# A gated hybrid decoder step: sampled values spread by selecting matmuls, and four state tiles

## The chip, the cores and the metric

The kernel runs on one core of a Trainium2 chip. The metric is the device time of one execution in microseconds (us); a timing is the median of several runs. The core has five engines with queues of their own that run beside each other and meet at semaphores: PE (TensorE, matmuls), DVE (VectorE), ACT (ScalarE), POOL (GpSimd, here mainly an issuer of DMAs) and SP (SyncE, the other issuer of DMAs). Each takes its instructions in order: one that waits holds those behind it.

## The reference

One layer of a decoder whose mixer has two branches on the same normalised input, retention and RWKV-7, for two sets of tokens: a prompt of 512 tokens that starts from zero states, and eight sampled tokens (one of each of eight sequences) that start from given states. All inputs and outputs are fp32.

```python
D_MODEL = 1024; SEQ = 512; DEC_BATCH = 8; RET_HEADS = 4; RET_DK = 256; RET_DV = 512

def chunk(s, qkv):                         # retention, one chunk of one head
    qc, kc, vc = qkv
    inner = jnp.einsum('bhid,bhjd->bhij', qc, kc) * dmask
    o = jnp.einsum('bhij,bhjv->bhiv', inner, vc) + jnp.einsum('bhid,bhdv->bhiv', qc * q_dec, s)
    s = chunk_dec * s + jnp.einsum('bhjd,bhjv->bhdv', kc * k_dec, vc)
    return s, o
...
o = o * lax.rsqrt(jnp.mean(o * o, axis=-1, keepdims=True) + NORM_EPS)
return o * jax.nn.silu(g_a), s             # the retention branch
...
def step(s, inp):                          # RWKV-7, one token
    r_t, w_t, k_t, v_t, kk_t, a_t = inp
    sk = jnp.einsum('bhvk,bhk->bhv', s, kk_t)
    s = s * w_t[:, :, None, :] - sk[..., None] * (a_t * kk_t)[:, :, None, :] + v_t[..., None] * k_t[:, :, None, :]
    return s, jnp.einsum('bhvk,bhk->bhv', s, r_t)
...
merged = sigmoid(m_a) * (y_a @ w_down_a) + sigmoid(m_b) * (y_b @ w_down_b)
x = x + merged @ w_out
x = x + (p @ w_ple) * sigmoid(_rmsnorm(x) @ w_ple_gate)
```

For a sampled token the retention state of one head, 256 by 512 values for each of eight sequences (4 MB), is multiplied by the head's decay, gets the outer product of the new key and value added, is written out, and is multiplied by the query. All eight states of four heads make 16 MB in and 16 MB out.

## The kernel before, in words

The work runs in three stages on one core. Stage A (to about 275 us) normalises and transposes the input, makes the RWKV projections and prepares per-chunk matrices, which it stores to memory. Stage B (to about 770 us) goes through the four retention heads. Stage C runs the RWKV chunks between the remaining projections, then the output projection, the gate and the final norm.

Every fp32 product is made as three fp32r products: an operand is split in a rounded part `hi` and a rest `lo`, and `hi·hi`, `hi·lo`, `lo·hi` are summed in PSUM. A weight block of 1024x128 is fetched by SP into one of three `raw` tiles, split by ACT (`whi`, L142) and DVE (`wlo`, L143), and used by 48 matmuls (L155), two halves of the tokens with 24 each, in four PSUM banks of the pool `ph`. One such block is called a projection here. Other results on PE go through three banks of the pool `px`, handed out by `bank()`; the sampled result has a bank `po` of its own.

A head in stage B makes, in this order in the code: the projections and rotation of k and q (two each, `rope`), four projections of v (`values`), the scores (`sc`, L776, split to `ihi` and `ilo`), transposes of v (`vt`, split to `vhi` and `vlo`), of the sampled v (`vs`) and of k (`kt`, split to `dhi` and `dlo`), the sampled states (`sampled`), four projections of the gate g_a (`gs`, in the slots of v), in the heads 2 and 3 also four projections of another gate, the output (`o`, L827, evacuated to `ot`), the new prompt state (`st`, L839), the transposes of `ot` (L846), the product with the gate (`y`, L848) and its store (`YAd`), and last `sampled_out`. The code's order is a priority, not the order on the engines: instructions are placed by a planner that simulates the engines and transfers ahead of time, each engine's list is fixed then, and the semaphores do the rest.

`sampled(h)` handles the 4 MB in four tiles of 1 MB: two groups `g` of four sequences, two halves `i` of the key dimension. Before the change the eight sampled value rows (512 values each) are written to memory (`VSd`, L797) and loaded again by a DMA that repeats them over all 128 partitions (`vb` in the tile `tv`, L690, 1 MB for each group, one slot, shared with `on` of `sampled_out`). The state tiles `tS` have two slots (L694); POOL issues their loads (L695) and stores (L705). ACT multiplies a tile by the decay (L698), DVE adds key times value (L699, with the key as the scalar of each partition), and PE multiplies by the query into `po` (L701). `after(m_, last)` makes the first of four po matmuls wait for the last state update before it.

Beside this, the generator `beside()` hands out DVE work in small pieces: first `solve()`, a triangular solve in the tile `M` (L615, L617) whose result is stored by SP (`TTd`), then `rwkv_sampled()`, which loads the RWKV states of the sampled tokens into the same slot `M` (L638) and updates them with nine DVE instructions for each of four parts (L643 to L660). `advance()` is called after each projection of k, q, v and g_a and takes pieces off the generator until a 42nd part of the whole work is paid for:

```python
def advance(share=1.0 / 42):
    nonlocal due
    due += share * WORK
    with tc.issue_after(marks[1]):
        while due > 0:
            w_ = next(extra, None)
            if w_ is None:
                break
            due -= w_ + 60
```

`issue_after(marks[1])` places those DVE instructions behind the latest weight split.

Of the kernel before, what the change touches and what calls it, by code (L numbers as in the profile page):

```python
# [8 lines left out]
F32 = mybir.dt.float32  # L9
F32R = mybir.dt.float32r  # L10
# [69 lines left out]
def body(tc, A, O, dbg=None, upto="Z"):  # L80
# [11 lines left out]
    with es:  # L92
# [24 lines left out]
        BNd = dr.tile([NPAIR, 128, NT], F32, tag="BNd", name="BNd")  # L117
        SMd = dr.tile([6, B8, D], F32, tag="SMd", name="SMd")
        OSd = dr.tile([128, 64], F32, tag="OSd", name="OSd")
        VSd = dr.tile([B8, H, DV], F32, tag="VSd", name="VSd")  # L120
        GBd = dr.tile([KT, 128, NT], F32, tag="GBd", name="GBd")
        UAd = dr.tile([KT, 128, NT], F32, tag="UAd", name="UAd")
        YBd = dr.tile([KT, 128, NT], F32, tag="YBd", name="YBd")
# [486 lines left out]
        def solve():  # L610
            for s in range(1, C - 1):
                n = C - 1 - s
                tm = pB.tile([128, 1024], F32, tag="tm", name="tm", bufs=1)
                tv = tm[:, 0:s * n].rearrange("p (i t) -> p i t", t=n)
                dve.tensor_tensor(tv, M[:, 0:s, s:s + 1].to_broadcast([128, s, n]),  # L615
                                  M[:, s:s + 1, s + 1:C].to_broadcast([128, s, n]), ALU.mult)
                dve.tensor_tensor(M[:, 0:s, s + 1:C], M[:, 0:s, s + 1:C], tv, ALU.add)  # L617
                yield s * n
            dve.memset(M.rearrange("p s t -> p (s t)")[:, 0::C + 1], 1.0)
            for c in range(NCH):  # L620
                sp.dma_start(TTd[c].rearrange("t h u -> h t u"), M[c * 16:(c + 1) * 16])
            yield 0
# [10 lines left out]
        def rwkv_sampled():  # L633
            S_ = pB.tile([128, C, C], F32, tag="M", name="S_")
            for q in range(C // HQ):
                vsl = slice(q * HQ, (q + 1) * HQ)
                S = S_[:, vsl]
                pool.dma_start(S, A["state_rwkv"][0].rearrange("b h v k -> (b h) v k")[:, vsl])  # L638
                tm = pB.tile([128, HQ, C], F32, tag="tm", name="rT", bufs=1)
                sk = pB.tile([128, HQ], F32, tag="rk", name="rk", bufs=1)  # L640
                kb = lambda i: sv[:, i:i + 1, :].to_broadcast([128, HQ, C])
                vb = lambda t: t.unsqueeze(2).to_broadcast([128, HQ, C])
                dve.tensor_tensor(tm, S, kb(4), ALU.mult)  # L643
                yield HQ * C / 2
                dve.tensor_reduce(sk, tm, AX.X, ALU.add)
                yield HQ * C / 2
                dve.tensor_tensor(S, S, kb(1), ALU.mult)
                yield HQ * C / 2
                dve.tensor_tensor(tm, vb(sk), kb(5), ALU.mult)
                yield HQ * C / 2  # L650
                dve.tensor_tensor(S, S, tm, ALU.subtract)
                yield HQ * C / 2
                dve.tensor_tensor(tm, vb(sv[:, 3, vsl]), kb(2), ALU.mult)
                yield HQ * C / 2
                dve.tensor_tensor(S, S, tm, ALU.add)
                yield HQ * C / 2
                pool.dma_start(O[6][0].rearrange("b h v k -> (b h) v k")[:, vsl], S)
                dve.tensor_tensor(tm, S, kb(0), ALU.mult)
                yield HQ * C / 2
                dve.tensor_reduce(os_[:, vsl], tm, AX.X, ALU.add)  # L660
                yield HQ * C / 2
            pool.dma_start(OSd, os_)

        def beside():
            yield from solve()
            yield from rwkv_sampled()

        extra = beside()
# [2 lines left out]
        def advance(share=1.0 / 42):  # L671
# [3 lines left out]
            with tc.issue_after(marks[1]):  # L675
                while due > 0:
# [2 lines left out]
                        break  # L679
                    due -= w_ + 60  # L680

        def sampled(h):
            qz = pR.tile([128, 2, 4, 34], F32, tag="qz", name="qz", bufs=1)
            dve.memset(qz, 0.0)
            dve.tensor_copy(qz[:, :, :, 0], qs[:, h, :, 0:4])
            dve.tensor_copy(qz[:, :, :, 33], qs[:, h, :, 4:8])
            po = pq.tile([128, 512], F32, tag="po", name="po")
            for g in range(2):
                vb = pR.tile([128, 4, DV], F32, tag="tv", name="tv", bufs=1)
                pool.dma_start(vb, VSd[4 * g:4 * g + 4, h, :].unsqueeze(0).to_broadcast([128, 4, DV]))  # L690
                for i in range(2):

                    src = slice(4 * g, 4 * g + 4)
                    S = pR.tile([128, 4, DV], F32, tag="tS", name="tS", bufs=2)  # L694
                    pool.dma_start(S, A["state_ret"][0, src, h, 128 * i:128 * i + 128, :].rearrange("b p v -> p b v"))  # L695
                    n_ = 32 if g == 0 and i == 0 else 2
                    for b in range(4):
                        act.activation(S[:, b, :], S[:, b, :], AF.Copy, scale=GAM[h])  # L698
                        last = dve.scalar_tensor_tensor(S[:, b, :], vb[:, b, :], ks[:, h, i, 4 * g + b:4 * g + b + 1], S[:, b, :], ALU.mult, ALU.add)  # L699
                    for b in range(4):  # L700
                        m_ = pe.matmul(po[32 * b:32 * b + n_, :], qz[:, i, b, 32 * g:32 * g + n_], S[:, b, :],  # L701
                                       start=(n_ == 32), stop=(g == 1 and i == 1), skip_group_check=True)
                        if b == 0:
                            after(m_, last)
                    pool.dma_start(O[5][0, src, h, 128 * i:128 * i + 128, :].rearrange("b p v -> p b v"), S)  # L705
            return po

        def sampled_out(h, po):
            on = pR.tile([128, DV], F32, tag="tv", name="on", bufs=1)
            os2 = small.tile([128, 2], F32, tag="os2", name="os2")  # L710
            act.activation(on, po, AF.Square, accum_out=os2[:, 0:1])
            rsqrt(os2[:, 1:2], os2[:, 0:1], 1.0 / DV, NORM_EPS)
            act.activation(on, po, AF.Copy, scale=os2[:, 1:2])
            ps = bank("yas")
            for i in range(4):
                pe.transpose(ps[:, 128 * i:128 * i + 128], on[:, 128 * i:128 * i + 128], ident)
            hs_ = slice(4 * h, 4 * h + 4)
            dve.tensor_tensor(yaS[:, hs_, :].rearrange("p i (g b) -> p i b g", g=2),
                              ps.rearrange("p (i b r) -> p i b r", i=4, b=4)[:, :, :, 0:2],
                              gs8[:, hs_, :].rearrange("p i (g b) -> p i b g", g=2), ALU.mult)  # L720
# [3 lines left out]
        for h in range(H):  # L724
# [61 lines left out]
            for jt in range(4):  # L786
                ps = bank("vt")
                for i in range(4):
                    pe.transpose(ps[:, 128 * i:128 * i + 128], vT[i][:, 128 * jt:128 * jt + 128], ident)
                act.activation(vhi[:, jt, :], ps, AF.Copy)  # L790
                dve.tensor_tensor(vlo[:, jt, :], ps, vhi[:, jt, :], ALU.subtract)
            ps = bank("vs")
            for i in range(4):
                pe.transpose(ps[0:B8, 128 * i:128 * i + 128], vT[i][:, T:NT], ident)
            vs = pB.tile([B8, DV], F32, tag="s_", name="vs", bufs=1)
            act.activation(vs, ps[0:B8, :], AF.Copy)
            pool.dma_start(VSd[:, h, :], vs)  # L797
            dhi = pB.tile([128, 4, 256], F32R, tag="khi", name="dhi")
            dlo = pB.tile([128, 4, 256], F32R, tag="klo", name="dlo")
            for jt in range(4):  # L800
# [17 lines left out]

            oss = pB.tile([128, 4], F32, tag="oss", name="oss", bufs=2)
            ort = pB.tile([128, 4], F32, tag="ort", name="ort", bufs=2)  # L820
            ot = []
            for it in range(4):
                ps = bank("o")
                seq = [(jt, a_, b_) for jt in range(it + 1) for a_, b_ in ((ihi, vhi), (ihi, vlo), (ilo, vhi))]
                for x, (jt, a_, b_) in enumerate(seq):
                    o_ = OFF[jt] + 128 * (it - jt)
                    pe.matmul(ps, a_[:, o_:o_ + 128], b_[:, jt, :], start=(x == 0), stop=(x == len(seq) - 1))  # L827
                o = pB.tile([128, DV], F32, tag="ot", name="ot", bufs=4)
                act.activation(o, ps, AF.Square, accum_out=oss[:, it:it + 1])
                act.activation(o, ps, AF.Copy)  # L830
                ot.append(o)
            rsqrt(ort, oss, 1.0 / DV, NORM_EPS)
            for it in range(4):
                act.activation(ot[it], ot[it], AF.Copy, scale=ort[:, it:it + 1])
# [8 lines left out]
            for i in range(4):  # L843
                ps = bank("ot")
                for it in range(4):
                    pe.transpose(ps[:, 128 * it:128 * it + 128], ot[it][:, 128 * i:128 * i + 128], ident)  # L846
                y = pB.tile([128, T], F32, tag="y", name="y", bufs=2)
                dve.tensor_tensor(y, ps, gs[i][:, 0:T], ALU.mult)  # L848
                sp.dma_start(YAd[4 * h + i], y)
            sampled_out(h, po)  # L850
        advance(1.0)
# [376 lines left out]
```

## Time and profile before

| | |
|---|---|
| median of three runs | 1140.19 us (1139.5 to 1141.54) |
| the profiled execution | 1142.53 us, span 1140.6 us |
| mean granted clock of PE | 0.969 |
| busy share PE, DVE, ACT, POOL | 93%, 68%, 44%, 6% |
| DMA | 211.1 MB, mean 185 GB/s |
| state loads, state stores, value loads | 16, 16 and 8 DMAs of 1 MB |

The profile is of one execution, slower than the median by 2.3 us. A row of the timeline gives the start, the duration, engine, line, operation, output and inputs, shapes and count, and in brackets the idle time of the engine before it and what ended that. A row of the table of waits gives who waited for whom, the total, the number of times and the longest. A row of the table of stretches gives start and end, length, busy time and number of instructions for each engine, then the granted clock of PE as a share of its full speed, the share of the DMA engines in use, and the rate in GB/s. PE matmuls overlap each other: their duration is longer than the distance of their starts, and the distance is what one costs.

### The profile page before, as it was taken

What the parts mean: (1) busy time and instruction counts of PE and PEld (TensorE: products, weight loads), DVE (VectorE), ACT (ScalarE), POOL (GpSimd) and SP (SyncE); (2) the same over time, 40 slices, a digit from 0 to 9 for tenths busy, and PEclk for the clock granted to TensorE, in tenths of its full rate; (3) what the DMA queues carried; (4) which work ended last, traced back from release to release, by engine and by line L of the source; (5) the groups of instructions that cost most, each with busy time, mean ns of one, the idle gap of its engine ahead of it and who ended that gap; (6) DMA issues with size and microseconds to landing.
All of it is one profiled execution on the core that took longest, in us unless ns stands there. A gap on an engine that the chain in (4) does not pass through costs nothing. (4 is left out here: it accounts for less than half of the span.)

```text
span 1140.6 us, 22817 instructions
## 1 busy us (share of the span) xinstructions
PE 1064.1 (93%) x9292; PEld 1014.4 (89%) x9292; DVE 781.2 (68%) x1429; ACT 505.0 (44%) x1035; POOL 69.9 (6%) x108
## 2 busy tenths in 40 slices
PE   7999998999899998989799998999999899999996
PEld 6999998999898898879788998899888798999995
DVE  6648887873697899877498854333779664566775
ACT  6745545553434453344335433433433223434554
POOL 2000000000101100100111001010000100000000
PEclk9999999999899999989899999999989999999998
DMA  5623686888725863675779436949997558852312
GB/s 176 182 75 95 145 201 161 213 220 235 258 83 136 244 230 86 159 265 167 199 206 353 157 95 165 298 154 313 321 288 244 159 157 227 270 149 93 92 58 76
DMA packets 255963, 211.10 MB, mean 185 GB/s; under 512 B 59444, under 2 KB 221089, under 8 KB 254706
## 3 DMA queue, kind: packets, MB, share of 16 engines
q1 hardware_dynamic: 240146, 153.27, 46.9%
q0 software_dynamic: 15552, 56.10, 16.0%
q8 instruction: 73, 1.20, 0.4%
q14 instruction: 32, 0.26, 0.1%
q10 hardware_dynamic: 160, 0.27, 0.1%
HBM read 147.67 MB, written 61.64 MB: 184 GB/s over the span
## 5 line engine op out<-in xcount | busy, mean ns | idle before, releaser
L155 PE MATMUL ph<-hhi,whi 128*128 128x256 f32 (+2 forms) x1552 | 448.6, 290 | 4.1 <-ACT gs L812 1.9
L155 PE MATMUL ph<-hhi,wlo 128*128 128x256 f32 (+2 forms) x1552 | 445.5, 289 | 6.2 <-DVE wlo L143 6.2
L155 PE MATMUL ph<-hlo,whi 128*128 128x256 f32 (+2 forms) x1552 | 446.9, 288 | 0.7 <-DVE hlo L277 0.6
L155 PEld LDWEIGHTS ph<-hhi,whi 128*128 128x128 f32 x1552 | 297.3, 192 | 11.4 <-issue 3.9
L155 PEld LDWEIGHTS ph<-hhi,wlo 128*128 128x128 f32 x1552 | 297.8, 192 | 9.0 <-DVE wlo L143 6.8
L155 PEld LDWEIGHTS ph<-hlo,whi 128*128 128x128 f32 x1552 | 297.8, 192 | 6.2 <-issue 4.3
L143 DVE TENSOR_TENSOR wlo<-raw,whi 128x1024 fp32r<-128x1024 f32 x135 | 164.9, 1222 | 94.0 <-ACT whi L142 92.8
L142 ACT ACTIVATE whi<-raw 128x1024 fp32r<-128x1024 f32 x135 | 142.7, 1057 | 181.8 <-PE ph L155 159.1
L155 PE MATMUL ph<-yahi,whi 128*128 128x256 f32 (+1 forms) x256 | 73.3, 295 | 2.8 <-ACT yahi L974 2.8
L155 PE MATMUL ph<-yalo,whi 128*128 128x256 f32 (+1 forms) x256 | 73.9, 293 | 0.0
L155 PE MATMUL ph<-yahi,wlo 128*128 128x264 f32 (+1 forms) x256 | 72.2, 291 | 0.0
L699 DVE SCALAR_TENSOR_TENSOR tS<-tv,ks,tS 128x512 f32<-128x512 f32 x64 | 44.1, 745 | 38.0 <-ACT tS L698 21.2
L615 DVE TENSOR_TENSOR tm<-M 128x62 f32<-128x62 f32 (+30 forms) x62 | 52.9, 854 | 12.3 <-DMA M<-XTd 11.7
L698 ACT ACTIVATE tS<-tS 128x512 f32<-128x512 f32 x64 | 35.0, 619 | 47.9 <-DMA tS<-in_state_ret_dram 47.4
L617 DVE TENSOR_TENSOR M<-M,tm 128x62 f32<-128x62 f32 (+30 forms) x62 | 52.9, 854 | 0.4
L155 PEld LDWEIGHTS ph<-yahi,whi 128*128 128x128 f32 x256 | 49.6, 197 | 3.6 <-ACT yahi L974 3.3
L155 PEld LDWEIGHTS ph<-yalo,whi 128*128 128x128 f32 x256 | 50.0, 196 | 0.3
L155 PEld LDWEIGHTS ph<-yahi,wlo 128*128 128x128 f32 x256 | 49.1, 195 | 0.2
L155 PE MATMUL ph<-ybhi,whi 128*128 128x256 f32 (+1 forms) x128 | 36.9, 290 | 1.6 <-ACT ybhi L1048 1.6
L155 PE MATMUL ph<-yblo,whi 128*128 128x264 f32 (+1 forms) x128 | 37.2, 291 | 1.3 <-DVE yblo L1049 1.3
L155 PE MATMUL ph<-ybhi,wlo 128*128 128x264 f32 (+1 forms) x128 | 36.7, 289 | 0.0
L155 PE MATMUL ph<-mglo,whi 128*128 128x264 f32 (+1 forms) x128 | 36.2, 283 | 0.0
(432 smaller groups left out, 1921.5 us busy)
## 6 DMA issues: line engine op xcount, KB each, us to landing
raw<-in_w_in_dram SPq DMA_DIRECT2D x97, 512.0 KB, 5.3
tS<-in_state_ret_dram POOLq DMA_DIRECT2D x16, 1024.0 KB, 11.1
out_dram<-tS POOLq DMA_DIRECT2D x16, 1024.0 KB, 6.1
tv<-VSd POOLq DMA_DIRECT2D x8, 1024.0 KB, 11.3
KR<-KRd SPq DMA_DIRECT2D x8, 1024.0 KB, 7.1
raw<-in_w_down_a_dram SPq DMA_DIRECT2D x16, 512.0 KB, 4.9
KRd<-KRS SPq DMA_DIRECT2D x16, 256.0 KB, 4.3
KRd<-GM SPq DMA_DIRECT2D x16, 256.0 KB, 3.2
```

Of the source, the lines that this page charges most:

```text
L142: cp = act.activation(hi, raw, AF.Copy)
L143: sb = dve.tensor_tensor(lo, raw, hi, ALU.subtract)
L155: m_ = pe.matmul(ps[:, 0:c1 - c0], w[:, k, :], r[:, k0 + k, c0:c1], start=(x == 0), stop=(x == n_ - 1))
L615: dve.tensor_tensor(tv, M[:, 0:s, s:s + 1].to_broadcast([128, s, n]), M[:, s:s + 1, s + 1:C].to_broadcast([128, s, n]), ALU.mult)
L617: dve.tensor_tensor(M[:, 0:s, s + 1:C], M[:, 0:s, s + 1:C], tv, ALU.add)
L698: act.activation(S[:, b, :], S[:, b, :], AF.Copy, scale=GAM[h])
L699: last = dve.scalar_tensor_tensor(S[:, b, :], vb[:, b, :], ks[:, h, i, 4 * g + b:4 * g + b + 1], S[:, b, :], ALU.mult, ALU.add)
```

## The change

The sampled values no longer go through memory. ACT evacuates the eight rows to the partitions 0 to 7 of `vsr` as fp32r, DVE writes the rest of the rounding to the partitions 32 to 39. `sel` holds, for each of the eight sequences, a 128x128 matrix whose rows b and 32+b are ones, so that one matmul with it puts row b, hi plus lo, on all 128 partitions of a bank. DVE then reads the value from PSUM. Both halves `i` of a group use the same bank, so the order within a group changes: both loads first, then per sequence one selecting matmul and two decays and updates, then all eight po matmuls and both stores. The wait put in by `after` stands once for each group, on the group's last update. `tS` has four slots, `on` has one of its own. `ot` moves into the slots of `qhi` and `qlo`, and `y` overwrites the gate `gs`, from which the store to `YAd` is made. Between `solve()` and `rwkv_sampled()` stands a pause worth two calls of `advance`.

```diff
@@ beside
             yield from solve()
+            yield 2 * WORK / 42
             yield from rwkv_sampled()
@@ before sampled
+        sel = pR.tile([128, B8, 128], F32R, tag="sel", name="sel")
+        pool.memset(sel.bitcast(F32), 0.0)
+        vsr = pR.tile([128, DV], F32R, tag="vsr", name="vsr")
+        pool.memset(vsr.bitcast(F32), 0.0)
+        for r0 in (0, 32):
+            act.activation(sel[r0:r0 + B8], ident[r0:r0 + B8, r0:r0 + B8].unsqueeze(2).to_broadcast([B8, B8, 128]), AF.Copy)
@@ sampled
             for g in range(2):
-                vb = pR.tile([128, 4, DV], F32, tag="tv", name="tv", bufs=1)
-                pool.dma_start(vb, VSd[4 * g:4 * g + 4, h, :].unsqueeze(0).to_broadcast([128, 4, DV]))
+                Ss = []
                 for i in range(2):
-                    src = slice(4 * g, 4 * g + 4)
-                    S = pR.tile([128, 4, DV], F32, tag="tS", name="tS", bufs=2)
-                    pool.dma_start(S, A["state_ret"][0, src, h, 128 * i:128 * i + 128, :].rearrange("b p v -> p b v"))
+                    S = pR.tile([128, 4, DV], F32, tag="tS", name="tS", bufs=4)
+                    pool.dma_start(S, A["state_ret"][0, 4 * g:4 * g + 4, h, 128 * i:128 * i + 128, :].rearrange("b p v -> p b v"))
+                    Ss.append(S)
+                for b in range(4):
+                    vb = bank("vb")
+                    pe.matmul(vb, sel[:, 4 * g + b, :], vsr, start=True, stop=True)
+                    for i, S in enumerate(Ss):
+                        act.activation(S[:, b, :], S[:, b, :], AF.Copy, scale=GAM[h])
+                        last = dve.scalar_tensor_tensor(S[:, b, :], vb, ks[:, h, i, 4 * g + b:4 * g + b + 1], S[:, b, :], ALU.mult, ALU.add)
+                for i, S in enumerate(Ss):
                     n_ = 32 if g == 0 and i == 0 else 2
-                    for b in range(4):
-                        act.activation(S[:, b, :], S[:, b, :], AF.Copy, scale=GAM[h])
-                        last = dve.scalar_tensor_tensor(S[:, b, :], vb[:, b, :], ks[:, h, i, 4 * g + b:4 * g + b + 1], S[:, b, :], ALU.mult, ALU.add)
                     for b in range(4):
                         m_ = pe.matmul(po[32 * b:32 * b + n_, :], qz[:, i, b, 32 * g:32 * g + n_], S[:, b, :],
                                        start=(n_ == 32), stop=(g == 1 and i == 1), skip_group_check=True)
-                        if b == 0:
+                        if b == 0 and i == 0:
                             after(m_, last)
...
@@ the head loop
             ps = bank("vs")
             for i in range(4):
                 pe.transpose(ps[0:B8, 128 * i:128 * i + 128], vT[i][:, T:NT], ident)
-            vs = pB.tile([B8, DV], F32, tag="s_", name="vs", bufs=1)
-            act.activation(vs, ps[0:B8, :], AF.Copy)
-            pool.dma_start(VSd[:, h, :], vs)
+            act.activation(vsr[0:B8], ps[0:B8, :], AF.Copy)
+            dve.tensor_tensor(vsr[32:32 + B8], ps[0:B8, :], vsr[0:B8], ALU.subtract)
...
-            ot = []
+            ot = [x[:, i, :] for x in (pB.tile([128, 2, DV], F32, tag=t, name="ot") for t in ("qhi", "qlo")) for i in range(2)]
...
-                o = pB.tile([128, DV], F32, tag="ot", name="ot", bufs=4)
+                o = ot[it]
...
-                y = pB.tile([128, T], F32, tag="y", name="y", bufs=2)
-                dve.tensor_tensor(y, ps, gs[i][:, 0:T], ALU.mult)
+                y = gs[i][:, 0:T]
+                dve.tensor_tensor(y, ps, y, ALU.mult)
                 sp.dma_start(YAd[4 * h + i], y)
```

More of the change, by code (lines that the diff above doesn't have):

```diff
@@ L119, in body @@
         OSd = dr.tile([128, 64], F32, tag="OSd", name="OSd")
-        VSd = dr.tile([B8, H, DV], F32, tag="VSd", name="VSd")
         GBd = dr.tile([KT, 128, NT], F32, tag="GBd", name="GBd")
@@ L702, in sampled @@
                                        start=(n_ == 32), stop=(g == 1 and i == 1), skip_group_check=True)
-                        if b == 0:
+                        if b == 0 and i == 0:
                             after(m_, last)
-                    pool.dma_start(O[5][0, src, h, 128 * i:128 * i + 128, :].rearrange("b p v -> p b v"), S)
+                    pool.dma_start(O[5][0, 4 * g:4 * g + 4, h, 128 * i:128 * i + 128, :].rearrange("b p v -> p b v"), S)
             return po
         def sampled_out(h, po):
-            on = pR.tile([128, DV], F32, tag="tv", name="on", bufs=1)
+            on = pR.tile([128, DV], F32, tag="on", name="on", bufs=1)
             os2 = small.tile([128, 2], F32, tag="os2", name="os2")
@@ L827, in body @@
                     pe.matmul(ps, a_[:, o_:o_ + 128], b_[:, jt, :], start=(x == 0), stop=(x == len(seq) - 1))
-                o = pB.tile([128, DV], F32, tag="ot", name="ot", bufs=4)
+                o = ot[it]
                 act.activation(o, ps, AF.Square, accum_out=oss[:, it:it + 1])
                 act.activation(o, ps, AF.Copy)
-                ot.append(o)
             rsqrt(ort, oss, 1.0 / DV, NORM_EPS)
```

## The prediction

> **What bounds the kernel now.** I read the page's busy times first, then a table of stretches, then who waited for whom on PE, and last the order of instructions around each wait.
>
> ```profile
> span 1140.6 us, 22817 instructions
> PE 1064.1 (93%) x9292; PEld 1014.4 (89%) x9292; DVE 781.2 (68%) x1429; ACT 505.0 (44%) x1035; POOL 69.9 (6%) x108
> ...
> core 0: us, PE busy (x) PEld busy (x) DVE busy (x) ACT busy (x) POOL busy (x), PEclk, DMA share, GB/s
> 345.00:450.00 105.00, 98.11 (x734) 90.18 (x732) 90.80 (x132) 47.92 (x97) 9.18 (x13) 0.98 0.59 176
> 450.00:550.00 100.00, 91.76 (x664) 82.91 (x665) 75.86 (x140) 43.82 (x94) 9.17 (x13) 0.95 0.66 187
> 550.00:660.00 110.00, 101.58 (x769) 94.19 (x768) 85.39 (x121) 47.81 (x97) 13.51 (x21) 0.95 0.74 235
> 660.00:770.00 110.00, 105.05 (x788) 97.83 (x787) 46.01 (x86) 43.58 (x87) 10.52 (x15) 0.97 0.60 178
> ```
>
> PE is busy 93% of the span, in the loop over the four heads (here from 345 us) too. A microsecond comes off only where PE idles or runs at a lower clock, and every added matmul is paid. DVE is second, 0.86 of the first stretch and 0.42 of the last. So I ask what PE waits for in the heads:
>
> ```profile
> PE po L701 <- DVE tS L699: 11.7, 4, 5.5
> PE kt L803 <- DVE vlo L791: 7.3, 1, 7.3
> PE vt L789 <- DVE vlo L791: 3.4, 2, 2.1
> PE ot L846 <- ACT ot L834: 2.2, 1, 2.2
> ```
>
> Columns: total, times, longest. The named releasers are only last links, so I follow each back:
>
> ```profile
> 491.16 2.19 ACT L698 ACTIVATE tS<-tS 128x512 f32<-128x512 f32 x4 [10.38 <-DMA tS<-in_state_ret_dram]
> ...
> 404.51 2.19 ACT L698 ACTIVATE tS<-tS 128x512 f32<-128x512 f32 x4 [4.81 <-DMA tS<-in_state_ret_dram]
> ...
> 700.66 5.39 DVE L699 SCALAR_TENSOR_TENSOR tS<-tv,ks,tS 128x512 f32<-128x512 f32 x8 [7.04 <-DMA tv<-VSd]
> ...
> 563.75 1.23 DVE L643 TENSOR_TENSOR rT<-S__6306,sv 128x1024 f32<-128x1024 f32 x1 [10.06 <-DMA S__6306<-in_state_rwkv_dram]
> ...
> tS<-in_state_ret_dram POOLq DMA_DIRECT2D x16, 1024.0 KB, 11.1
> out_dram<-tS POOLq DMA_DIRECT2D x16, 1024.0 KB, 6.1
> tv<-VSd POOLq DMA_DIRECT2D x8, 1024.0 KB, 11.3
> ```
>
> The bracket is the idle time before the instruction and what ended it. All are late DMAs. The longest wait at po (5.5 us) ends behind DVE, behind ACT, which stood 10.38 us, until 491, at a state tile still loading. At 404 ACT stands the same way, and the scaling of ot queued behind it (the 2.2 us wait at L846) is late. At 700 DVE stands 7.04 us at tv. At 563 DVE stands 10.06 us at the RWKV state; vlo is queued behind, and kt waits 7.3 us for vlo. A state load takes 11.1 us and can start only after an output of 6.1 us frees one of two slots; tv takes 11.3 us in its single slot.
>
> Waiting also costs clock. The stretches around the four longest of these waits at po and kt (PE busy, clock), then two matmul starts at full clock:
>
> ```profile
> 489.00:501.00 12.00, 6.48 (x37) 0.72 0.68 250
> 556.00:572.00 16.00, 8.66 (x55) 0.68 0.82 257
> 700.00:709.00 9.00, 5.83 (x35) 0.81 0.56 194
> 724.00:733.00 9.00, 7.21 (x47) 0.81 0.97 311
> ...
> 502.08 0.28 PE L155 MATMUL ph<-hhi,whi 128*128 128x264 f32 x1
> 502.20 0.28 PE L155 MATMUL ph<-hlo,whi 128*128 128x264 f32 x1
> ```
>
> At 0.72 or 0.68 of the clock PE does less even where it is busy. At full clock starts are 0.12 us apart.
>
> **The change, part by part.**
>
> *State tiles two to four, tv and VSd gone.* Eight loads of 11.3 us and four stores leave POOL's queue. All state tiles of a head fit at once, and those of the next head load while this one's projections run, far more than 11.1 us ahead. The po waits (11.7) and the ot wait (2.2) lose their cause: −13.9 us. Had other work late on DVE caused them, this would be nothing; the rows above say DMA. What is late next is DVE itself, priced under the new waits.
>
> *Pause of two steps before the sampled RWKV.* One advance follows each projection of 48 matmuls at 0.12 us, 5.8 us, so its first DVE instruction moves behind at least 11.6 us of PE work. Its wait was 10.06 us and shrinks to nothing: kt no longer waits, −7.3 us. The DVE work itself only moves, into the last stretch where DVE has 64 us free.
>
> *Clock.* The lost clock of the four stretches is length times (1 − clock) times PE's busy share: 12 × 0.28 × 0.54 = 1.8, 16 × 0.32 × 0.54 = 2.8, 9 × 0.19 × 0.65 = 1.1, 9 × 0.19 × 0.80 = 1.4; together −7.1 us.
> [...]
>
> *Selecting matmuls.* Eight a head, 32 in all, fp32r 128x512 with 128 weights, as the o matmuls:
>
> ```profile
> 362.79 0.40 PE L827 MATMUL o<-vhi,ilo 128*128 128x512 f32 x1
> ...
> 364.19 0.40 PE L827 MATMUL o<-vhi,ilo 128*128 128x512 f32 x1
> ...
> L791 DVE TENSOR_TENSOR vlo<-vt,vhi 128x512 fp32r<-128x512 f32 x16 | 10.8, 685 | 4.2 <-ACT vhi L790 4.2
> ...
> L744 DVE TENSOR_TENSOR qlo<-m,qhi 128x512 fp32r<-128x512 f32 x8 | 5.5, 684 | 0.0
> ```
>
> Six steps in 1.40 us, 0.233 each: +7.5 us, nothing hides it. DVE gains four subtractions of about 0.685 us, one a head: 2.7 us, hidden under PE as long as DVE is not the releaser; without that cover, 2.7 us. The 64 state updates now read their values from PSUM. Reading PSUM cost L791 nothing beside L744, which reads SBUF (685 against 684 ns): I take 0.
> [...]
>
> *New waits.* vb takes one of three PSUM banks of the ring x and holds it until two state updates are done. Eight updates in 5.39 us make 1.35 us a pair. From below 0. From above: of a head's eight vb, five must wait for an earlier pair, each 1.35 − 0.23 = 1.1 us, 5.6 us a head, 22.4 in all, if PE has nothing between them. But the projections of g_a are ready between them (four banks of their own). The nearest row is vt, which cycles through the same banks behind ACT and DVE: 3.4 us of wait over 16 tiles, so 6.8 over 32. I take 6.8, keeping 0 and 22.4. The wait that orders po behind the last update of its group remains; I count it there.
>
> *Four state loads at the start instead of two.* They come just when DMA is full (the stretch's row, and the row of an issue needed just below):
>
> ```profile
> 270.00:300.00 30.00, 25.09 (x202) 24.83 (x201) 7.43 (x14) 6.77 (x13) 5.20 (x9) 0.92 0.98 307
> ...
> YAd<-y SPq DMA_DIRECT2D x16, 256.0 KB, 3.3
> ```
>
> Two more MB at 307 GB/s are 6.8 us of delay at most for the weights queued beside them, 0 at least, since three weight tiles are fetched ahead. I take 2.
>
> *In place, and set-up.* y no longer needs a slot of its own; its price is that the next head's vT waits for the landing of YAd. Between lie four projections (k and q, 23 us): 0, if PE's order keeps that; without this cover, the median landing of 3.3 us at three borders, 10 us. ot in the slots of qhi and qlo makes the next q wait for the transposes of ot: 0 for the same reason. Building sel is two ACT copies of 8x1024 and POOL memsets, in the stretch above where ACT was busy 6.77 of 30 us: 0, and at worst a copy that stands on ACT behind POOL, whose queue is held by earlier loads; it would delay the weights behind it.
>
> *Sum:* −13.9 − 7.3 − 7.1 + 7.5 + 6.8 + 2 = −12.0 us. The profiled execution took 1142.5 us, 1.9 beyond its span, so 1130.5; it lies 2.3 above the median of 1140.19, so the forecast is 1128 us.
>
> **The rivals.**
>
> 1. *Nothing new is waited for.* The projections cover every bank: −28.3 + 7.5 = −20.8, 1119 us. For it: 23 us of g_a projections a head. Against: DVE fills 0.86 of the first stretch, and each projection needs a wlo from it.
>
> 2. *PE stands in order behind vb.* A vb is queued on PE ahead of projections that don't need it, and holds them until DVE frees a bank. With the upper price: −28.3 + 7.5 + 22.4 + 2 + 3 of clock = +6.6, about 1147 us. It decides against the change once waits at vb pass 20 us in total. For it: PE does stand 11.7 us at po, with ready projections queued behind. Against: those stands came from DMA, which vb doesn't depend on by itself.
>
> 3. *Only the pause helps.* DVE's order behind state updates makes po as late as before: −7.3 − 2.8 + 7.5 = −2.6, 1138 us. Against: DVE stood idle for 7.04 us just before the updates at 700 us, so it was not short of time.
>
> 4. *The time is the same:* the whole order is planned again, and new waits, at vb or elsewhere, eat the 20.8 us: 1140.
>
> **How the numbers follow.** Forecast 0.36, rival 1 0.25, rival 3 0.12, rival 4 0.12, rival 2 0.15. Within 0.2% (2.3 us) a measurement of this kernel cannot be told from no change. So faster 0.73, same 0.12, slower 0.15. The range runs from 1115 us (rival 1 and the 3.4 us at vt gone as well) to 1142 (past rival 4), and leaves out rival 2; the forecast's own range is 1121 to 1136 us.
>
> **What would show it.** Right: no idle before L698 or the state updates ended by a state DMA, first RWKV product without a wait for its load, PE's wait at kt gone, 32 vb matmuls about 0.23 us apart from their neighbours, waits at vb and po below 10 us together, clock above 0.97 from 345 to 770 us. Wrong: PE idle before vb of over 20 us; or weights late after 290 us; or PE gaps at vT, waiting for YAd.

## The result, and the profile after

The changed kernel took 1122.84 us (median of 4 runs, 1120.05 to 1124.49) beside 1140.87 us for the kernel before on the same chip: ratio 0.9849, 95% interval 0.9816 to 0.9881. In a second comparison (e12 below) the ratio was 0.9857 (0.982 to 0.9893). The forecast was 1128 us in a range of 1115 to 1142, 12.0 us less than before. The two medians are 18.0 us apart, so the outcome lies between the forecast and rival 1 (20.8 us less), and nearer to the rival. The profiled execution took 1122.57 us.

The page of the changed kernel: span, busy times, the group of the state updates, and the state DMAs.

```profile
span 1120.8 us, 22849 instructions
PE 1066.7 (95%) x9324; PEld 1018.3 (91%) x9324; DVE 786.1 (70%) x1433; ACT 508.1 (45%) x1037; POOL 63.0 (6%) x98
...
L707 DVE SCALAR_TENSOR_TENSOR tS<-vb,ks,tS 128x512 f32<-128x512 f32 x64 | 43.9, 745 | 3.1 <-PE vb L704 3.1
...
L706 ACT ACTIVATE tS<-tS 128x512 f32<-128x512 f32 x64 | 35.1, 622 | 4.5 <-DMA tS<-in_state_ret_dram 4.3
...
tS<-in_state_ret_dram POOLq DMA_DIRECT2D x16, 1024.0 KB, 8.4
out_dram<-tS POOLq DMA_DIRECT2D x16, 1024.0 KB, 7.8
```

The share of PE rose from 93% to 95%. Before the 64 state updates DVE now stands 3.1 us, all behind a selecting matmul, and ACT 4.3 us at loading states. In the kernel before, the groups from 345 to 780 us have this pair for DVE and ACT (in each: busy us, mean ns | idle just before, by what ended it):

```profile
L699 DVE SCALAR_TENSOR_TENSOR tS<-tv,ks,tS 128x512 f32<-128x512 f32 x64 | 44.1, 745 | 38.0 <-ACT tS L698 21.2 <-DMA tv<-VSd 16.7
L698 ACT ACTIVATE tS<-tS 128x512 f32<-128x512 f32 x56 | 30.7, 619 | 47.9 <-DMA tS<-in_state_ret_dram 47.4 <-DVE tS L699 0.5
```

So DVE's 38.0 us of standing became 3.1, and ACT's 47.4 became 4.3. What PE waits for in the heads of the changed kernel (total, times, longest):

```profile
PE vt L800 <- DVE vlo L802: 6.0, 3, 2.8
PE ph L154 <- ACT gs L823: 2.4, 1, 2.4
PE ph L154 <- ACT vT L764: 1.9, 1, 1.9
PE ot L856 <- DVE gs L858: 1.1, 1, 1.1
```

No wait at po, kt or vb is left. The table of stretches of the changed kernel, to be set beside the four rows of before in the prediction (the last row already holds the start of stage C):

```profile
345.00:450.00 105.00, 99.51 (x732) 92.36 (x733) 96.87 (x140) 45.99 (x95) 7.12 (x10) 0.97 0.48 156
450.00:550.00 100.00, 96.03 (x721) 88.55 (x719) 72.59 (x136) 47.54 (x99) 9.24 (x14) 0.98 0.65 201
550.00:660.00 110.00, 110.00 (x840) 103.57 (x839) 88.72 (x125) 49.91 (x101) 9.87 (x15) 0.98 0.58 196
660.00:770.00 110.00, 110.00 (x1014) 103.05 (x1014) 50.96 (x94) 43.38 (x86) 6.43 (x9) 1.00 0.64 198
```

PE's busy time in these 425 us went from 98.11 + 91.76 + 101.58 + 105.05 = 396.5 to 415.5 us: 19 us less idle time. Lost clock, as the sum of busy time times (1 − clock), went from 2.0 + 4.6 + 5.1 + 3.2 = 14.8 to 3.0 + 1.9 + 2.2 + 0 = 7.1: 7.7 us less. The selecting matmuls take 7.5 of it back, so 19.2 us should be won here. Ahead of the heads there is a smaller gain; the same stretch before and after:

```profile
270.00:345.00 75.00, 70.09 (x561) 69.56 (x560) 49.90 (x78) 28.45 (x55) 5.20 (x9) 0.95 0.61 188
```

```profile
270.00:345.00 75.00, 69.82 (x572) 68.85 (x570) 52.80 (x81) 36.40 (x68) 8.06 (x13) 1.00 0.66 212
```

With 0.05 more clock on 70 us that is 3.5 us, less 0.3 us of busy time, so 3.2 us, though two more state tiles are loaded in it (the DMA share is 0.66 instead of 0.61). Part of this belongs to the single execution: the same kernel profiled again (e12) had a clock of 0.98 there. The first weight load of the RWKV chunks marks the start of stage C (first and last start stand behind the durations), before and after:

```profile
L931 PEld LDWEIGHTS UO<-SV,KR x512: 132/138/139, 775.7 to 904.4; 128*64 128x64 f32 x171
```

```profile
L941 PEld LDWEIGHTS UO<-SV,KR x512: 132/138/138, 752.5 to 883.9; 128*64 128x64 f32 x171
```

It comes 23.2 us earlier, near the 19.2 + 3.2 = 22.4 us of the two sums. The rest of the span takes 368.3 us instead of 364.9, so 3.4 us are given back in stage C.

### The profile page after: what moved, and what is told of

It is laid out like the page before. It is cut to its first block, busy times and chain, and to the rows that moved or that the text cites. A ratio compares the mean times of both kernels' runs of the same rounds, so it can differ in the third digit from the quotient of the medians.

```text
span 1120.8 us, 22849 instructions
## 1 busy us (share of the span) xinstructions
PE 1066.7 (95%) x9324; PEld 1018.3 (91%) x9324; DVE 786.1 (70%) x1433; ACT 508.1 (45%) x1037; POOL 63.0 (6%) x98
## 4 chain that ended last, share of the span: by engine, by line
PE 79%; DMA 10%; DVE 6%; ACT 3%; issue 1%; SPq 0%; POOL 0%; DVEq 0%; POOLq 0%; ACTq 0%
PE ph L154 64%; DMA ya<-YAd 3%; PE o L838 3%; PE st L849 2%; PE g L498 2%; PE po L712 1%; DMA yb<-BNd 1%; DVE wlo L142 1%; ACT whi L141 1%; PE sc L787 1%; DMA YBd<-yb 1%; DMA raw<-in_w_in_dram 1%; DMA BKt<-BKd 1%; PE vb L704 1%; DMA xt<-in_x_prompt_dram 1%
## 5 line engine op out<-in xcount | busy, mean ns | idle before, releaser
L154 PE MATMUL ph<-yahi,wlo 128*128 128x256 f32 (+1 forms) x256 | 74.0, 295 | 0.1
L707 DVE SCALAR_TENSOR_TENSOR tS<-vb,ks,tS 128x512 f32<-128x512 f32 x64 | 43.9, 745 | 3.1 <-PE vb L704 3.1
```

The source lines that it names most:

```text
L154: m_ = pe.matmul(ps[:, 0:c1 - c0], w[:, k, :], r[:, k0 + k, c0:c1], start=(x == 0), stop=(x == n_ - 1))
L707: last = dve.scalar_tensor_tensor(S[:, b, :], vb, ks[:, h, i, 4 * g + b:4 * g + b + 1], S[:, b, :], ALU.mult, ALU.add)
```

## The experiments

All ratios are to the kernel before on the same chip, in five rounds, with a 95% interval. A trace is of one execution and can lie off the median: it took 1154.05 us in e3, 1152.14 in e5, 1139.1 in e4 and 1123.05 in e7. Its waits therefore show where an engine stands and are not added up to the difference of two medians. Theory A is the prediction's: late transfers held DVE and ACT, the pause moves the wait for the RWKV state, each selecting matmul is paid. Most rivals give the gain to one part alone.

### The pause alone, and the change without it

e1 is the kernel before with one line, e2 the changed kernel without it:

```diff
             yield from solve()
+            yield 2 * WORK / 42
             yield from rwkv_sampled()
```

> The kernel before with the pause of two steps alone. Theory A (each part of the change removes the waits that the trace of before shows, each by itself): the 10.06 us stand of DVE at the RWKV state and the 7.3 us wait of PE at kt go, with 2.8 us of clock; about 10 us faster than before, near 1130 us; the waits at po stay near 11.7 us. Rival B (what counts is that the planner lays the whole order out anew; the parts do nothing by themselves): any time within a few us of 1140 us, with a new wait in the place of the old one.

> The changed kernel without the pause. Theory A: the stand of DVE at the RWKV state (10 us) and PE's wait at kt (7 us) come back, 1122.8 + 7.3 + 2.8, near 1133 us. Rival C (with four state tiles and no value loads the transfers are light enough that the RWKV state is in time anyway): within 3 us of 1123 us.

Measured: e1 1138.19 us, 0.9994 (0.9971 to 1.0016); e2 1119.27 us, 0.9828 (0.9799 to 0.9857). The pause of two does nothing by itself, as rival B had it, and the change does without it: e2 comes near the time that rival C gave it. Rows of e1: PE's waits, and DVE's wait for the RWKV state:

```profile
PE po L702 <- DVE tS L700: 16.3, 8, 5.4
PE kt L804 <- DVE vlo L792: 5.8, 1, 5.8
```

```profile
DVE rT L643 <- DMA S__6424<-in_state_rwkv_dram: 8.5, 1, 8.5
```

The stand of 10.06 us is still 8.5, and kt still waits 5.8 us of its 7.3. The pause of two took little of either. Now DVE's wait in e2, without a pause, and in the changed kernel, with it:

```profile
DVE rT L642 <- DMA S__6321<-in_state_rwkv_dram: 6.5, 1, 6.5
```

```profile
DVE rT L642 <- DMA S__6439<-in_state_rwkv_dram: 6.0, 1, 6.0
```

The two stand almost alike, so C's cause, a state that is in time, isn't there. What PE pays for it changed more than the stand: kt's wait of 7.3 us in before and 5.8 us in e1 is 0.4 us in e2, and vt waits somewhat longer than its 3.4 us in before:

```profile
PE vt L799 <- DVE vlo L801: 6.5, 3, 3.2
...
PE kt L813 <- DVE vlo L801: 0.4, 1, 0.4
```

### State tiles and the way of the values, each alone

e3 is the changed kernel with two tiles; e4 is before with four tiles and the edits in place, the values still through memory; e6 is before with the edits in place alone.

```diff
@@ e3, against the changed kernel
-  S = pR.tile([128, 4, DV], F32, tag="tS", name="tS", bufs=4)
+  S = pR.tile([128, 4, DV], F32, tag="tS", name="tS", bufs=2)
@@ e4, against before (and e6's edits)
-  S = pR.tile([128, 4, DV], F32, tag="tS", name="tS", bufs=2)
+  S = pR.tile([128, 4, DV], F32, tag="tS", name="tS", bufs=4)
@@ e6, against before
-  ot = []
+  ot = [x[:, i, :] for x in (pB.tile([128, 2, DV], F32, tag=t, name="ot") for t in ("qhi", "qlo")) for i in range(2)]
...
-  y = pB.tile([128, T], F32, tag="y", name="y", bufs=2)
-  dve.tensor_tensor(y, ps, gs[i][:, 0:T], ALU.mult)
+  y = gs[i][:, 0:T]
+  dve.tensor_tensor(y, ps, y, ALU.mult)
```

> The changed kernel with two state tiles in place of four, all else kept, the selecting matmuls too. Theory A (the late state loads are the cause of the waits at po): a load starts again only after a store has freed its slot, so ACT stands at tS again, the updates are late and po or vb waits for them: 8 to 14 us of waits with some clock, 1133 to 1140 us. Rival D (the late value loads were the cause, and the matmuls alone cure them): within 4 us of 1123 us.

> The kernel before with the outputs in place (which makes the room) and four state tiles; values still through memory in one slot, no pause. Theory A: ACT stands at tS no more; what is left of the waits at po is what the value loads cost (the value tile of the second group can load only after the updates of the first, 11.3 us): 11.7 falls to about 5, the wait at ot goes, 2 us of clock: near 1130 us. Rival D (value loads alone are the cause): 1138 to 1141 us, waits at po unchanged.

> The kernel before with the outputs in place alone. Theory A: the projections of k and q cover the landing of YAd and the transposes of ot; within 2.5 us of the kernel before, 1138 to 1142 us. Rival E: ACT's vT waits for the landing at each border of heads, and PE behind it, up to 10 us slower, 1145 to 1150 us.

Measured: e3 1146.25 us, 1.0061 (1.0033 to 1.0089); e4 1134.36 us, 0.996 (0.9936 to 0.9983); e6 1133.73 us, 0.9956 (0.9932 to 0.998). With e2 they make a table, all with the edits in place (e3 also has the pause, which e1 puts at nothing):

| | values through memory | selecting matmuls |
|---|---|---|
| two state tiles | 0.9956 (e6) | 1.0061 (e3) |
| four state tiles | 0.9960 (e4) | 0.9828 (e2) |

Four tiles are worth nothing while the values go through memory and 2.3% with the matmuls; the matmuls cost 1.05% with two tiles and win 1.3% with four. e3 is slower than either of its theories allowed, and e4 lies between its two. The right column also has the new order inside a group (all po matmuls behind all updates), which no run has without the matmuls, so what the order does alone isn't shown. Why the left column doesn't move: in e4, DVE's wait in the heads and PE's behind it.

```profile
DVE tS L699 <- DMA tv<-VSd: 45.5, 8, 12.4
```

```profile
PE po L701 <- DVE tS L699: 17.6, 5, 5.2
```

No update waits behind ACT any more, and DVE now stands 45.5 us at the one slot of tv; before it was 38.0 at both. The late value loads had in part been hidden behind the late states. The reverse does not hold: in e3, without the value loads, DVE stands only 11.7 us before its updates, and PE has no wait at po. The updates, ACT's groups and PE's waits there:

```profile
L707 DVE SCALAR_TENSOR_TENSOR tS<-vb,ks,tS 128x512 f32<-128x512 f32 x64 | 44.2, 744 | 11.7 <-ACT tS L706 9.3 <-PE vb L704 2.4
...
L706 ACT ACTIVATE tS<-tS 128x512 f32<-128x512 f32 x56 | 30.7, 621 | 11.4 <-DMA tS<-in_state_ret_dram 9.1 <-DVE nt L179 2.3
...
L764 ACT ACTIVATE vT<-ph 128x256 f32<-128x256 f32 (+1 forms) x24 | 8.7, 380 | 24.0 <-PE ph L154 13.2 <-DMA YAd<-gs 10.8
```

```profile
PE ph L154 <- ACT vT L764: 11.5, 2, 10.1
PE ot L856 <- ACT ot L844: 8.3, 1, 8.3
```

ACT stands only 9.1 us at states (47.4 in before). What the matmuls won at po is lost elsewhere: PE is held at the borders of heads, 10.1 us where the next v waits for the store of y out of the gate's slots (the price that the prediction named for "in place" if its cover is gone), and 8.3 where the scaling of ot is late.

e6 gains 0.44% (5.0 us, 2.3 to 7.7 by the interval). The likely cause is a row of the kernel before: DVE stood at the two slots of y.

```profile
DVE y L848 <- DMA YAd<-y: 7.6, 2, 5.0
```

The same product and the next head's vT in e6:

```profile
L847 DVE TENSOR_TENSOR gs<-ot,gs 128x512 f32<-128x512 f32 x16 | 10.4, 684 | 7.6 <-PE ot L845 7.6
...
L753 ACT ACTIVATE vT<-ph 128x256 f32<-128x256 f32 (+1 forms) x24 | 9.0, 378 | 13.4 <-PE ph L155 12.0 <-DMA YAd<-gs 1.4
```

With the product written over the gate, DVE no longer waits for the store; 1.4 us come back as ACT's wait at vT.

### The matmuls with two tiles, and three attempts on their cost

e5 is before with the selecting matmuls and their order inside a group alone (two tiles, ot and y in their own slots, no pause).

> The kernel before with the selecting matmuls alone: two state tiles, ot and y in tiles of their own, no pause. Theory A (value loads and state loads both late; curing one leaves the other): the waits ended by a state load stay (8 to 10 us at po or ot), the one ended by a value load goes (3.2 us), the matmuls cost 7.5 us: 1140 to 1146 us. Rival E (the loss with two tiles and outputs in place came from the outputs in place, since vT waited 10.8 us there for the store of YAd): clearly below the time of that kernel, 1130 to 1138 us.

Measured: 1147.18 us, 1.0078 (1.005 to 1.0105), so slower, and as slow as e3: what holds e3 back is not the edits in place, which rival E blamed. PE's longest waits, and the stretch at the first border of heads in e5 and in before:

```profile
PE sc L786 <- ACT qhi L753: 9.0, 1, 9.0
PE ot L856 <- ACT ot L844: 8.3, 1, 8.3
```

```profile
400.00:430.00 30.00, 19.85 (x112) 17.07 (x109) 28.39 (x48) 15.45 (x33) 2.29 (x4) 0.79 0.39 136
```

```profile
400.00:430.00 30.00, 27.84 (x233) 27.60 (x232) 27.40 (x47) 16.13 (x33) 0.76 (x1) 1.00 0.64 212
```

PE idles a third of that stretch while DVE is nearly full. In before the o products of the first head ran between its two groups of state updates, from 362 us on (the prediction's rows). In e5 their first result is taken only at 393 us:

```profile
393.29 0.60 ACT L840 ACTIVATE ot<-o 128x512 f32<-128x512 f32 x1 [2.93 <-PE o L837]
```

The 8.3 us at ot can be followed from there. ACT takes the last o at 404.15 us; the small DVE instructions of its norm then run from 404.87 to 422.97 us, between pieces of `solve()` and other work, and ACT scales ot at 423.01. In the changed kernel the same chain runs from 388.87 on, and ot is scaled at 407.88. I took the late o for the cause of the loss (theory H): the output waits for o, o waits for vb, vb for the second group's states. Two kernels, both made from e5, tested it: e9 puts `po = sampled(h)` behind the o loop, e10 gives vb a bank of the projections' ring and leaves the order.

```diff
@@ e9 and e11: the call moved
-            po = sampled(h)
...
             (the loop over o)
+            po = sampled(h)
@@ e10
-                    vb = bank("vb")
+                    vb = ph.tile([128, 512], F32, tag="h", name="vb")
```

> The kernel with selecting matmuls and two state tiles only, with the selecting matmuls moved behind the o products in the order of TensorE. Theory H (two tiles and selecting matmuls cost 7 to 9 us over before because the o products stand behind the second group's selecting matmuls, which wait for VectorE and the state loads): o runs between the groups again as in before, the scaling of o near 423 no longer waits, the time is 1130 to 1139. Rival I (the stall at the border of two heads is VectorE's own load there, whatever o does): 1144 to 1149 and the wait at the transposition of the output stays near 8 us.

> The kernel with selecting matmuls and two state tiles only, with the results of the selecting matmuls in the ring of banks that the projections' products use, not in the ring of o; the order in the program is unchanged. Theory H1 (o is late because it shares the three banks of that ring with the selecting matmuls): o interleaves with them, 1130 to 1140. Rival H2 (o is late by its place in the order alone, or the stall is VectorE's load): 1143 to 1149; TensorE would then stand before projection products for banks that VectorE hasn't read.

Measured: e9 1173.22 us, 1.0324 (1.0296 to 1.0352); e10 1173.97 us, 1.0312 (1.0278 to 1.0346). Both are slower than e5, by 2.3 to 2.5%, and than any of their theories allowed; as an account of the lost time theory H is not borne out. In e9 the 8.3 us at ot did go, as H said, but others came; a PE wait, and the groups in which DVE and ACT stand at the store of y:

```profile
PE ph L154 <- ACT vT L763: 6.6, 1, 6.6
```

```profile
L763 ACT ACTIVATE vT<-ph 128x256 f32<-128x256 f32 (+1 forms) x24 | 8.5, 377 | 18.7 <-DVE y L857 16.0 <-PE ph L154 2.7
L857 DVE TENSOR_TENSOR y<-ot,gs 128x512 f32<-128x512 f32 x12 | 8.2, 688 | 14.2 <-DMA YAd<-y 13.7 <-PE ot L855 0.6
```

And the sampled work of a head, now its last, ends later: the evacuation of po in e5, then in e9 (first and last start):

```profile
L721 ACT ACTIVATE on<-po x4: 597/600/602, 400.3 to 746.7; 128x512 f32<-128x512 f32 x4
```

```profile
L721 ACT ACTIVATE on<-po x4: 597/597/597, 410.3 to 794.6; 128x512 f32<-128x512 f32 x4
```

The last is 48 us later, and the RWKV chunks start at 814.1 instead of 784.6 us. In e10 PE stands where the rival of H put it, at projections whose bank a vb still holds while its state loads:

```profile
PE ph L154 <- DVE tS L706: 23.7, 4, 7.6
```

```profile
L706 DVE SCALAR_TENSOR_TENSOR tS<-vb,ks,tS 128x512 f32<-128x512 f32 x64 | 43.9, 743 | 16.8 <-ACT tS L705 16.5 <-PE vb L703 0.2
L705 ACT ACTIVATE tS<-tS 128x512 f32<-128x512 f32 x56 | 30.7, 618 | 24.0 <-DMA tS<-in_state_ret_dram 21.7 <-DVE ort L180 1.7 <-DVE nt L178 0.5
```

With four tiles the changed kernel has no such wait at either ring. So the late o explains the wait at ot, but what e5 and e3 lose in all is not settled. Every kernel here is an order planned anew, and moving o alone brought other waits. How much of each ratio is the luck of an order no run separates; the change, e2, e7, e8 and e11, which all have four tiles and the matmuls, are all below 1, at 0.9794 to 0.9923.

### The price of a selecting matmul

e7 issues every selecting matmul of the changed kernel twice into the same bank.

```diff
-                    pe.matmul(vb, sel[:, 4 * g + b, :], vsr, start=True, stop=True)
+                    for _ in range(2):
+                        pe.matmul(vb, sel[:, 4 * g + b, :], vsr, start=True, stop=True)
```

> The changed kernel with each selecting matmul made twice into the same bank, 32 more matmuls that change no result. Theory A (every matmul on PE is paid in full, nothing hides it): 32 x 0.233 = 7.5 us more than the changed kernel, near 1130 us, and no wait of PE at vb. Rival F (PE has idle time around the sampled states, which takes them up): less than 3 us more, 1123 to 1126 us.

Measured: 1130.22 us, 0.9923 (0.9895 to 0.995). Against the changed kernel's 0.9849 that is 0.74% or 8.4 us for 32 matmuls, with an uncertainty of about 5 us from the two intervals; 7.5 was expected. The two kernels ran on different chips. A vb in the changed kernel's timeline steps as the o products did:

```profile
373.11 0.40 PE L704 MATMUL vb<-vsr,sel 128*128 128x512 f32 x1
373.35 0.28 PE L154 MATMUL ph<-hhi,wlo 128*128 128x264 f32 x1
```

0.24 us from start to start.

### A longer pause, the later o, and the change again

e8 is the changed kernel with a pause of 7 calls of `advance` instead of 2, e11 that with the call moved behind the o loop, e12 the changed kernel as it is, on one chip with e9 to e11.

> The changed kernel with a pause of seven calls instead of two: the planner then places the first RWKV product on DVE behind the k transposes of that head, some 15 us of work later, where a pause of two left it in its place. Theory A, mended (a pause helps if it moves that product past the landing of its load): DVE's stand of 6.0 us at the load goes and with it PE's 2.75 us at vt and 1.5 us of clock, near 1119 us. Rival G (DVE has so much to do later that the product is as much in the way there): 1121 to 1126 us.

> The changed kernel, all four state tiles, with a pause of 7 calls and the selecting matmuls behind the o products. If the place of o matters with four tiles too: 1108 to 1114, below the pause of 7 alone (1114.66 when measured). If four tiles have already freed o (it follows at 375, right behind the last of 16 subtractions): 1113 to 1117, the same as the pause of 7 alone. If the output norm then waits for the later values: above 1118.

> The changed kernel as it is, beside before and the others on one chip: ratio 0.984 to 0.988 if the first comparison holds (0.9849), 1120 to 1125 us; the difference to the pause of 7 with late selecting matmuls then tells what the last two edits are worth together (6 to 10 us if each run so far holds).

Measured: e8 1114.66 us, 0.9794 (0.9757 to 0.9831); e11 1126.76 us, 0.9908 (0.9879 to 0.9936); e12 1121.21 us, 0.9857 (0.982 to 0.9893). In e8 DVE no longer stands at the RWKV state. The first and last start of the RWKV product in the changed kernel and in e8, then PE's stretch in e8, full at full clock:

```profile
L642 DVE TENSOR_TENSOR rT<-S__6439,sv x4: 1216/1221/1226, 547.7 to 637.3; 128x1024 f32<-128x1024 f32 x4
...
L642 DVE TENSOR_TENSOR rT<-S__6926,sv x4: 1209/1218/1219, 556.2 to 664.4; 128x1024 f32<-128x1024 f32 x4
...
550.00:660.00 110.00, 110.00 (x851) 103.67 (x850) 76.25 (x113) 49.75 (x102) 8.25 (x12) 1.00 0.58 194
```

In the changed kernel POOL issues the loads from 541.1 us on, and they land 6.6 to 9.7 us after their issue: the product starts 6.6 us after the first issue, as long as the shortest of these landings. In e8 it starts 8.5 us later than there, and DVE has no idle time before it that a load ends. A pause of seven takes DVE's stand away, as the prediction wanted; one of two did not. e8 is the lowest ratio measured, but its interval overlaps with those of e2 and of the change, so that it beats them isn't shown; nor was it run on one chip with them. Moving the call costs here too: e11, on another chip, lost 1.1% against e8. Its last po evacuation starts at 747 us (698.5 in the changed kernel) and the RWKV chunks at 766.8 (752.5).

## Why the prediction was nearly right, step by step

- **What bounds it.** Right: PE's idle time and clock in the heads. 19 us of idle time and 7.7 us of clock went, and time went with them.
- **State tiles and tv (−13.9).** The po waits went altogether, and DVE's idle time before L707 ended by a DMA is none. But the step gave the gain to "the state tiles" and "tv" in one term without saying that neither alone is worth anything in time: e4 left 17.6 us at po; e3 has no wait at po, but it waits at the borders of heads and was slower than before.
- **Pause (−7.3).** Wrong as a step. It said that rT "moves behind at least 11.6 us of PE work"; in e1 the stand only shrank from 10.06 to 8.5 us, and kt still waited 5.8 us. The step took the pause for a delay between a load and its use; in the whole change the product starts at 547.7 us with a pause of two and at 546.2 without one (e2), and DVE's stand with it (6.0 us) is nearly that without it (6.5 us). The kt wait did go with the rest of the change, with 2.8 us at vt in its place at most; that it went while the named cause stayed was luck for this term. In e7, whose code differs by 32 matmuls alone, kt waits 4.4 us again.
- **Clock (−7.1).** Right: −7.7 in the heads, 14.8 us lost before and 7.1 after. The step took the clock as measured around each wait, 0.68 to 0.81; the changed kernel still has four dips to 0.81 in the heads (below).
- **Selecting matmuls (+7.5).** Right: 0.24 us a step, 8.4 us by e7. The DVE updates show no price for reading PSUM: 745 ns from PSUM at L707, 745 ns from SBUF at L699 before.
- **New waits at vb (+6.8 of 0 to 22.4).** The mis-sized term: PE has no wait at vb. The near row, vt behind DVE, was the wrong neighbour: in the timeline above a projection's matmuls (ph) follow a vb at once, so PE has other work between two vb. The vt row itself rose, from 3.4 to 6.0 us, which the sum didn't have. In e7, with twice as many, there is no wait at vb either. The lower bound was the right one; that is rival 1's case.
- **Loads at the start (+2 of 0 to 6.8).** None seen: PE's one wait for weights there is 3.2 us, against 4.9 in before, and the stretch from 270 to 345 us did 3.2 us more.
- **In place (0).** Off: the prediction weighed only its price and not what it removes. It is worth 0.44% alone (e6), and a wait of 7.6 us that it removes stood in the profile. Its price shows too: in the changed kernel PE waits 1.9 us behind a vT that waits for the store.
- **Not foreseen:** 3.4 us given back in stage C. PE is busy 342.8 us there instead of 339.7, at the same clock of 0.96; why is open.

The sum was 6 us short of the gain because errors in both directions partly cancelled. The vb waits and the loads were too dear by 8.8 us and in place was left out; against them stand stage C and the rise at vt. The pause's term came out only because its wait went with other parts of the change. So the nearness of the total is partly luck. Rival 3, only the pause helps, is refuted by e1; rival 2's price at vb shows nowhere in the change, but e10 shows how it looks: 23.7 us at the banks that vb holds, with two tiles.

## What to carry to other kernels

When a wait ends with one of two late transfers, cost each half and the pair. Here more slots alone left DVE standing for the other transfer (45.5 us in e4), the matmuls alone took most of the stand away (11.7 us left of 38.0 in e3) but brought waits elsewhere (10.1 and 8.3 us in e3, 9.0 and 8.3 in e5), and only both together, with the pause or without it, are worth 1.4 to 1.7%. Look for idle time before an instruction that writes into a slot whose store is still running: here it was 7.6 us at y, and overwriting the input removed it (e6). Whether a pause takes a stand away is read from the landing of the load and the consumer's start, not from the number of calls: with two calls the product still started 6.6 us after the first issue of its loads and DVE stood 6.0 us, with seven it started 8.5 us later and without a stand.

## What was not expected of the hardware

Not every wait of PE in the changed kernel costs clock. Five stretches of 9 us around the changed kernel's longest waits (length, PE busy, clock, DMA share, GB/s):

```profile
292.00:301.00 9.00, 5.82 (x49) 1.00 0.94 338
343.00:352.00 9.00, 6.57 (x43) 0.81 0.21 60
414.00:423.00 9.00, 6.01 (x37) 0.81 0.53 176
448.00:457.00 9.00, 5.99 (x36) 0.81 0.30 87
547.00:556.00 9.00, 6.46 (x42) 0.81 0.55 211
```

PE's idle time, 9 us less its busy time, is 2.4 to 3.0 us in the last four, and each has a clock of 0.81, so 1.1 to 1.2 us lost as busy time times (1 − clock); the 3.2 us at 292 to 301, one single wait, cost none. In these rows the length of a wait does not tell by itself whether it costs clock.
